# A hybrid GLA and DeltaNet layer: a substitution's transfers on GpSimd's queue, and a reordered last scaling

## The chip, the cores and the metric

The kernel runs on one core of one Trainium2 chip. The metric is the device time of one execution in microseconds (us); the median of several executions counts. The core has five engines that run their own instruction lists in order: PE (TensorE, matrix products, with its weight loads shown as PEld), DVE (VectorE), ACT (ScalarE), POOL (GpSimd) and SP (SyncE). SP, ACT and POOL can also issue transfers (DMA); such an issue stands in the engine's own list, and an issue that has to wait holds back whatever stands behind it on that engine.

## The reference, cut to what matters

```python
h = rms_norm(x, g_mix); z = h @ w_in                       # 256 tokens, 2048 channels
o_gla = gla_mixer(...)                                     # 4 heads
# gated delta rule, 16 heads, chunks of 64 tokens
a = where(strict, (k_beta @ k.T) * decay, 0)
t_mat = triangular_solve(eye + a, eye, lower, unit_diagonal)
u, w = t_mat @ (v * beta), t_mat @ (k_beta * exp(gcum))    # then a scan over the chunks
x = x + mixed @ w_out
x = x + square(relu(rms_norm(x, g_mlp) @ w_up)) @ w_down
x = x + sigmoid(rms_norm(x, g_ple) @ w_ple_gate) * (p @ w_ple_proj)
out = rms_norm(x, g_final)                                 # x * rsqrt(mean(x*x)+eps) * g_final
```

## The kernel before, in words

All matrix products keep fp32 accuracy by splitting each operand into two parts. A helper, `weights`, loads 1 MB of weights into a tile `raw` (line 93, issued by SP), rounds it to `whi` on ACT (line 101) and subtracts to `wlo` on DVE (line 102). One such pair of tiles feeds one group of matmuls: in `stream` 12 matmuls of 512 columns (lines 114 to 116). There are three buffers each of `raw`, `whi` and `wlo`, so ACT and DVE can be three groups ahead of PE and no more. A matmul on line 114 needs `whi` of its group, the next one, on line 115, needs `wlo`.

The mixers run in four passes of the loop over `h` (line 353), each with one GLA head and four DeltaNet heads. In each pass the inverse of the triangular matrices is built from 32x32 diagonal blocks, for which the kernel does a forward substitution with one block per partition (lines 465 to 492):

- Four transfers (line 468) write the diagonal blocks of the tile `af` to a DRAM tile `da`; one (line 470) reads it back as `a32`, which is a slice of the buffer `cacc`.
- 62 small DVE instructions (lines 479 and 481) do the substitution into `t32`, between the DVE work of the streams; a copy (line 483) puts the transposed result into `cacc` again.
- `t32` goes to DRAM as `dt` (line 484), the copy as `du` (line 485); from there two transfers fill `t11` (line 491), four `u_bd` (line 489), one `tb` (line 492). These are read by small matmuls (lines 574 and 582) some 40 us later.

The buffer `cacc` exists once. Its next user is the convolution of the same pass's V: `qkv("v", ...)` starts it with four ACT instructions (line 378), each followed by three DVE instructions (line 381, 12 in all), which end in one ACT instruction (line 384). So line 378 cannot start before the transfer `du` has read `cacc`, that is, before it has landed.

At the end (lines 808 to 845) the gate product is done for 512 columns at a time, the last 512 columns for each half of the tokens in two blocks of 256 columns (96 matmuls of 256 columns for each 128 tokens). `gated` evacuates a block: sigmoid on ACT (801), two DVE instructions (802, 803), a sum of squares on ACT (804), and a DVE product with `gfin` (806), the final gain. Then the sum, the root on POOL (178), four scalings by it, two on DVE (844) and two on ACT (842), and four transfers out by SP (845).

The order of the instructions on each engine is set at build time by a scheduler that works with its own estimates of durations. Where an instruction is given to another engine, the scheduler also orders the others anew.

Of the kernel before, what the change touches and what calls it, by code (L numbers as in the profile page):

```python
# [12 lines left out]
AF = mybir.ActivationFunctionType  # L13
ALU = mybir.AluOpType
AX = mybir.AxisListType
# [3 lines left out]
D = 2048  # L19
# [18 lines left out]
def hybrid_block(ctx: ExitStack, tc: tile.TileContext, A: dict, out: bass.AP):  # L38
    nc = tc.nc
    V, SC, GP, TE, SY = nc.vector, nc.scalar, nc.gpsimd, nc.tensor, nc.sync  # L40
# [27 lines left out]
    def mm():  # L68

        return psm.tile([P, 2, 512], F32, tag="mm", name="mm")  # L70
# [4 lines left out]
    def T4(tag, bufs=None, dt=F32):  # L75
        return mp.tile([P, 4, S], dt, tag=tag, bufs=bufs, name=tag)
# [98 lines left out]
    def rsqrt_(dst, src, mul, tmp):  # L175

        V.tensor_scalar(tmp, src, mul, EPS, ALU.mult, ALU.add)
        GP.tensor_tensor(dst, tmp, mhalf[:, :dst.shape[1]], ALU.pow)
# [101 lines left out]
    rtmp = const.tile([P, NT], F32, name="rtmp")  # L280
# [18 lines left out]
    u_bd = mp.tile([P, 8, P], F32, name="u_bd")  # L299
    t11 = mp.tile([64, 8, 64], F32, name="t11")  # L300
# [52 lines left out]
    for h in range(GH):  # L353
# [58 lines left out]
        for i, src in enumerate((kT, qT)):  # L412
            for t in range(NT):
# [4 lines left out]
                for hd in range(4):  # L418
                    c = i * 8 + t * 4 + hd
# [22 lines left out]
        af = T4("af").rearrange("p a (b c) -> p (a b) c", b=2)  # L442
        for t in range(NT):
            ts = slice(t * P, (t + 1) * P)
# [20 lines left out]
        da, dt_, du = (dram.tile([32, 32, 32], F32, name=n) for n in ("da", "dt", "du"))  # L465
        for b in range(4):
            bs = slice(b * 32, (b + 1) * 32)
            SC.dma_start(da[b * 8:(b + 1) * 8].rearrange("i s c -> s i c"), af[bs, :, bs])
        a32 = T4("cacc")[0:32].rearrange("p a b -> p (a b)").rearrange("p (s c) -> p s c", s=32)
        SC.dma_start(a32, da)  # L470
        t32 = mp.tile([P, NT, 512], F32, tag="og", name="t32").rearrange("p a b -> p (a b)")[0:32]
        GP.memset(t32, 0.0)
        GP.memset(t32[:, 0:1024:33], 1.0)
        t32 = t32.rearrange("p (c s) -> p c s", c=32)
        tmp = mp.tile([P, 8, 32], F32, tag="tmp", name="tmp").rearrange("p a b -> p (a b)")[0:32]
        for j in range(31):
            n, m = 31 - j, j + 1
# [3 lines left out]
            V.tensor_tensor(t32[:, j + 1:, 0:m], t32[:, j + 1:, 0:m], tv, ALU.subtract)  # L481
        u32 = a32
        V.tensor_copy(u32, t32.rearrange("p c s -> p s c"))
        SC.dma_start(dt_, t32)
        SC.dma_start(du, u32)
        tb = mp.tile([P, 8, 32], F32, tag="tmp", name="tb")
        for b in range(4):
            bs, ds = slice(b * 32, (b + 1) * 32), slice(b * 8, (b + 1) * 8)
            SC.dma_start(u_bd[bs, :, bs], du[ds].rearrange("i s c -> s i c"))  # L489
            if b < 2:  # L490
                SC.dma_start(t11[bs, :, bs], dt_[ds].rearrange("i c s -> c i s"))
        SC.dma_start(tb[64:96], dt_[16:24].rearrange("i c s -> c i s"))

        vT = qkv("v", O_DV, 32)
        rv = mp.tile([P, NT, 4, P], F32, name="rv")
# [30 lines left out]
        for t in range(NT):  # L526
            ts = slice(t * P, (t + 1) * P)
# [153 lines left out]
        for kp in range(2):  # L681
            pz = mx3(2, S)
            for kk in range(2):
                for t in range(NT):
                    c = (kp * 2 + kk) * P
# [8 lines left out]
    x_sb = late.tile([P, NT, D], F32, name="x_sb")  # L694
# [79 lines left out]
    gfin = late.tile([P, D], F32, name="gfin")  # L774
# [12 lines left out]
    def ple_proj(n):  # L787
        pj = [None, None]

        def ev(t, ps):  # L790
            pj[t] = late.tile([P, 512], F32, tag=f"pj{t}", name="pj")
            SC.activation(pj[t], ps, AF.Copy)

        stream([w_pp[:, n * 512:(n + 1) * 512]], 2, pT, ev)
        return pj

    def gated(t, c, n, ps, pj, i):

        xs = x_sb[:, t, c:c + n]
        s = late.tile([P, 512], F32, tag="u", bufs=2, name="s")[:, 0:n]  # L800
        SC.activation(s, ps, AF.Sigmoid, scale=r3[:, t:t + 1])
        V.tensor_tensor(s, s, pj, ALU.mult)
        V.tensor_tensor(xs, xs, s, ALU.add)
        SC.activation(late.tile([P, 512], F32, tag="junk", name="junk")[:, 0:n], xs, AF.Square,
                      accum_out=ssf[:, t, i:i + 1])
        V.tensor_tensor(xs, xs, gfin[:, c:c + n], ALU.mult)

    ssf = late.tile([P, NT, 5], F32, name="ssf")
    for n in range(3):
        pj = ple_proj(n)  # L810
        stream([w_pg[:, n * 512:(n + 1) * 512]], KD, h3T,
               lambda t, ps: gated(t, n * 512, 512, ps, pj[t], n))


    pj = ple_proj(3)
# [8 lines left out]
    ssl = late.tile([P, NT], F32, name="ssl")  # L824
    r4 = late.tile([P, NT], F32, name="r4")
    for t in range(NT):
        ts = slice(t * P, (t + 1) * P)
        for half in range(2):
            cs = slice(half * 256, (half + 1) * 256)
            ps = mm()[:, 0, 0:256]  # L830
            for k in range(KD):
                hi, lo = kept[k]
                TE.matmul(ps, h3T[0][:, k, ts], hi[:, cs], start=(k == 0), stop=False)
                TE.matmul(ps, h3T[0][:, k, ts], lo[:, cs], start=False, stop=False)
                TE.matmul(ps, h3T[1][:, k, ts], hi[:, cs], start=False, stop=(k == KD - 1))
            gated(t, 1536 + half * 256, 256, ps, pj[t][:, cs], 3 + half)
        V.reduce_sum(ssl[:, t:t + 1], ssf[:, t, :], axis=AX.X)
        rsqrt_(r4[:, t:t + 1], ssl[:, t:t + 1], 1.0 / D, rtmp[:, t:t + 1])
        for n in range(4):
            xs = x_sb[:, t, n * 512:(n + 1) * 512]  # L840
            if n % 2:
                SC.activation(xs, xs, AF.Copy, scale=r4[:, t:t + 1])
            else:
                V.tensor_scalar(xs, xs, r4[:, t:t + 1], None, ALU.mult)
            SY.dma_start(out[0, ts, n * 512:(n + 1) * 512], xs)


_INS = ["x", "p", "g_mix", "w_in", "gla_w2", "gla_b", "gla_norm", "dn_conv", "dn_a_log", "dn_dt_bias", "dn_norm",
# [19 lines left out]
```

## Time and profile before

| | |
|---|---|
| median of 3 runs | 1858.05 us (1855.92 to 1859.32) |
| the profiled execution | 1857.95 us, of which the span of the instructions is 1856.2 us |
| PE busy | 1827.8 us, 98% of the span |
| DVE, ACT, POOL busy | 64%, 51%, 4% |
| DMA | 334 MB, 180 GB/s in the mean |

The span is what the views of the trace show; 1.75 us of the execution lie outside it. PE's busy time is the sum of its records, whose ends are modelled; matmuls follow each other faster than one record lasts, so what PE loses is best read from the starts of neighbouring matmuls. PEclk is the granted clock of TensorE, 1.00 being 2.4 GHz.

### The profile page before, as it was taken

Reading aid. Unit: us, or ns where it says so; the run is one execution under the profiler, and the core shown is the slowest. Engines: PE = TensorE matmul, PEld = TensorE weight load, DVE = VectorE, ACT = ScalarE, POOL = GpSimd, SP = SyncE. Lnnn points to the kernel's source line nnn. Section 1 sums busy time; section 2 is a strip of 40 time slices with the busy share of each in tenths; the row PEclk is TensorE's granted clock in tenths of the full one; section 3 lists DMA queues with packets and bytes.
Section 4 is the critical chain, followed back from the end, with each engine's and each line's share of the span. In section 5 each row is a group of like instructions: output and inputs, shape, how many; then the busy total and the mean of one; then the engine's idle time right before and its main releaser. Section 6 shows DMA issues by size and latency. Waiting matters only on the chain.

```text
span 1856.2 us, 24598 instructions
## 1 busy us (share of the span) xinstructions
PE 1827.8 (98%) x9796; PEld 1551.0 (84%) x9796; DVE 1180.2 (64%) x1637; ACT 946.6 (51%) x1324; POOL 77.5 (4%) x100
## 2 busy tenths in 40 slices
PE   8999999999999999999999999999999999999998
PEld 7887888878888788887888888888888888888887
DVE  5686577864768647686455655555556555565665
ACT  6745556455564655645545544444444434344654
POOL 3110011000110001100000000000000000000000
PEclk9999999999999999999999999999999999999999
DMA  7555446554455545565465665656656565655453
GB/s 239 148 185 169 159 149 192 168 172 160 155 179 187 178 150 159 159 205 167 144 233 191 184 192 182 198 187 188 196 183 194 191 190 193 187 188 195 162 201 137
DMA packets 245236, 334.02 MB, mean 180 GB/s; under 512 B 21680, under 2 KB 148992, under 8 KB 244736
## 3 DMA queue, kind: packets, MB, share of 16 engines
q1 hardware_dynamic: 231488, 325.47, 54.4%
q10 hardware_dynamic: 12992, 4.34, 1.0%
q0 software_dynamic: 640, 2.63, 0.4%
q8 instruction: 77, 1.26, 0.3%
q14 instruction: 39, 0.32, 0.0%
HBM read 328.74 MB, written 3.67 MB: 179 GB/s over the span
## 4 chain that ended last, share of the span: by engine, by line
PE 92%; DMA 3%; DVE 2%; ACT 2%; issue 1%; ACTq 1%; SPq 0%; POOLq 0%; POOL 0%; DVEq 0%
PE mm L131 24%; PE mm L115 16%; PE mm L116 16%; PE mm L114 16%; PE mm L135 13%; DMA du<-cacc 1%; DMA raw<-in_w_in 1%; PE mx L457 1%; DMA x_sb<-in_x 1%; DVE wlo L102 1%; ACT whi L101 1%; DVE cacc L381 1%; PE mx L562 0%; PE mx L168 0%; ACTq L489 0%
## 5 line engine op out<-in xcount | busy, mean ns | idle before, releaser
L102 DVE TENSOR_TENSOR wlo<-raw,whi 128x1024 fp32r<-128x1024 f32 x604 | 743.8, 1234 | 532.0 <-ACT whi L101 523.3
L101 ACT ACTIVATE whi<-raw 128x1024 fp32r<-128x1024 f32 x604 | 638.8, 1060 | 746.5 <-PE mm L116 389.3
L131 PE MATMUL mm<-act,whi 128*128 128x512 f32 x1984 | 542.7, 395 | 0.0
L131 PEld LDWEIGHTS mm<-act,whi 128*128 128x128 f32 x1984 | 339.7, 189 | 45.8
L115 PE MATMUL mm<-wlo,act 128*128 128x512 f32 x864 | 343.1, 397 | 8.9 <-DVE wlo L102 8.9
L114 PE MATMUL mm<-whi,act 128*128 128x512 f32 x864 | 339.2, 393 | 3.2 <-ACT whi L101 3.2
L135 PEld LDWEIGHTS mm<-act,wlo 128*128 128x128 f32 x1984 | 304.0, 189 | 43.0 <-issue 1.0
L116 PE MATMUL mm<-whi,act 128*128 128x512 f32 x864 | 338.9, 392 | 0.0
L135 PE MATMUL mm<-act,wlo 128*128 128x256 f32 x1984 | 317.4, 281 | 0.0
L115 PEld LDWEIGHTS mm<-wlo,act 128*128 128x128 f32 x864 | 163.1, 189 | 44.0 <-DVE wlo L102 10.4
L116 PE MATMUL mm<-whi,ul 128*128 128x512 f32 x512 | 199.6, 390 | 0.0
L114 PE MATMUL mm<-whi,uh 128*128 128x512 f32 x512 | 199.5, 390 | 0.0
L115 PE MATMUL mm<-wlo,uh 128*128 128x512 f32 x512 | 199.3, 389 | 0.0
L114 PEld LDWEIGHTS mm<-whi,act 128*128 128x128 f32 x864 | 162.8, 188 | 38.3 <-ACT whi L101 4.9
L116 PEld LDWEIGHTS mm<-whi,act 128*128 128x128 f32 x864 | 163.1, 189 | 33.7 <-issue 1.0
L116 PEld LDWEIGHTS mm<-whi,ul 128*128 128x128 f32 x512 | 96.1, 188 | 19.9
L115 PEld LDWEIGHTS mm<-wlo,uh 128*128 128x128 f32 x512 | 96.1, 188 | 19.8
L114 PEld LDWEIGHTS mm<-whi,uh 128*128 128x128 f32 x512 | 96.1, 188 | 19.6
L381 DVE SCALAR_TENSOR_TENSOR cacc<-zT,convw,cacc 128x255 f32<-128x255 f32 (+2 forms) x144 | 61.0, 477 | 18.0 <-ACT cacc L378 18.0
L757 DVE SCALAR_TENSOR_TENSOR x_sb<-mm,r2sq,x_sb 128x512 f32<-128x512 f32 x64 | 45.1, 746 | 12.2 <-PE mm L116 12.2
L479 DVE TENSOR_TENSOR tmp<-cacc,t 32x31 f32<-32x31 f32 (+15 forms) x124 | 40.6, 328 | 4.4 <-DMA cacc<-da 1.5
L481 DVE TENSOR_TENSOR t<-t,tmp 32x31 f32<-32x31 f32 (+15 forms) x124 | 40.8, 329 | 2.8
(311 smaller groups left out, 1230.6 us busy)
## 6 DMA issues: line engine op xcount, KB each, us to landing
raw<-in_w_in SPq DMA_DIRECT2D x143, 1024.0 KB, 4.9
raw<-in_w_up SPq DMA_DIRECT2D x64, 1024.0 KB, 5.6
raw<-in_w_down SPq DMA_DIRECT2D x64, 1024.0 KB, 4.9
raw<-in_w_out SPq DMA_DIRECT2D x16, 1024.0 KB, 4.9
raw<-in_w_ple_gate SPq DMA_DIRECT2D x16, 1024.0 KB, 4.9
x_sb<-in_x POOLq DMA_DIRECT2D x1, 2048.0 KB, 12.4
raw<-in_w_ple_proj SPq DMA_DIRECT2D x4, 512.0 KB, 3.8
out<-x_sb SPq DMA_DIRECT2D x8, 256.0 KB, 2.5
```

The costliest lines, as they stand in the source:

```text
L101: SC.activation(hi[:, :, :c], raw[:, kk:kk + g, :c], AF.Copy)
L102: V.tensor_tensor(lo[:, :, :c], raw[:, kk:kk + g, :c], hi[:, :, :c].bitcast(F32), ALU.subtract)
L114: TE.matmul(pt[:, t, :n], xh[:, k, ts], hi, start=(k == 0), stop=False)
L115: TE.matmul(pt[:, t, :n], xh[:, k, ts], lo, start=False, stop=False)
L116: TE.matmul(pt[:, t, :n], xl[:, k, ts], hi, start=False, stop=(k == nk - 1))
L131: TE.matmul(pt[c // 2][:, c % 2, :], hi[:, c * P:(c + 1) * P], xx[:, k].rearrange("p a s -> p (a s)"), start=(k == 0), stop=False)
L135: TE.matmul(pt[c // 2][:, c % 2, S:2 * S], lo[:, c * P:(c + 1) * P], xh[:, k, :], start=False, stop=(k == nk - 1))
L381: V.scalar_tensor_tensor(acc[:, hd, sh:], zt[:, hd, :S - sh], w(i), acc[:, hd, sh:], ALU.mult, ALU.add)
L457: TE.matmul(pk[:, hd, :], kT[:, hd, ts], rhs[:, hd, ts], start=True, stop=True)
L479: V.tensor_tensor(tv, a32[:, j, j + 1:].unsqueeze(2).to_broadcast([32, n, m]), t32[:, j, 0:m].unsqueeze(1).to_broadcast([32, n, m]), ALU.mult)
L481: V.tensor_tensor(t32[:, j + 1:, 0:m], t32[:, j + 1:, 0:m], tv, ALU.subtract)
L757: V.scalar_tensor_tensor(x_sb[:, t, ns], ps, r2sq[:, t:t + 1], x_sb[:, t, ns], ALU.mult, ALU.add)
```

## The change

All transfers of the substitution are issued by GpSimd (`GP`) and no longer by ScalarE (`SC`). In the last part the first 128 tokens take the last 512 columns in one block. The gain `g_final` is no longer multiplied in by `gated` for the last columns (all 512 of the first 128 tokens, the last 256 of the second); one DVE instruction does the root and the gain together for these, and is first in the last scaling. The four scalings and four transfers out are put in another order, and one of the four is issued by ACT.

```diff
-            SC.dma_start(da[b * 8:(b + 1) * 8].rearrange("i s c -> s i c"), af[bs, :, bs])
+            GP.dma_start(da[b * 8:(b + 1) * 8].rearrange("i s c -> s i c"), af[bs, :, bs])
         a32 = T4("cacc")[0:32].rearrange("p a b -> p (a b)").rearrange("p (s c) -> p s c", s=32)
-        SC.dma_start(a32, da)
+        GP.dma_start(a32, da)
...
         V.tensor_copy(u32, t32.rearrange("p c s -> p s c"))
-        SC.dma_start(dt_, t32)
-        SC.dma_start(du, u32)
+        GP.dma_start(dt_, t32)
+        GP.dma_start(du, u32)
...
-            SC.dma_start(u_bd[bs, :, bs], du[ds].rearrange("i s c -> s i c"))
+            GP.dma_start(u_bd[bs, :, bs], du[ds].rearrange("i s c -> s i c"))
             if b < 2:
-                SC.dma_start(t11[bs, :, bs], dt_[ds].rearrange("i c s -> c i s"))
-        SC.dma_start(tb[64:96], dt_[16:24].rearrange("i c s -> c i s"))
+                GP.dma_start(t11[bs, :, bs], dt_[ds].rearrange("i c s -> c i s"))
+        GP.dma_start(tb[64:96], dt_[16:24].rearrange("i c s -> c i s"))
...
-        V.tensor_tensor(xs, xs, gfin[:, c:c + n], ALU.mult)
+        if gain:
+            V.tensor_tensor(xs, xs, gfin[:, c:c + n], ALU.mult)
...
-        for half in range(2):
-            cs = slice(half * 256, (half + 1) * 256)
-            ps = mm()[:, 0, 0:256]
+        w = 256 if t else 512
+        for i, c in enumerate(range(0, 512, w)):
+            cs = slice(c, c + w)
+            ps = mm()[:, 0, 0:w]
...
-            gated(t, 1536 + half * 256, 256, ps, pj[t][:, cs], 3 + half)
-        V.reduce_sum(ssl[:, t:t + 1], ssf[:, t, :], axis=AX.X)
-        rsqrt_(r4[:, t:t + 1], ssl[:, t:t + 1], 1.0 / D, rtmp[:, t:t + 1])
-        for n in range(4):
-            xs = x_sb[:, t, n * 512:(n + 1) * 512]
-            if n % 2:
-                SC.activation(xs, xs, AF.Copy, scale=r4[:, t:t + 1])
+            gated(t, 1536 + c, w, ps, pj[t][:, cs], 3 + i, gain=c < 256 and t == 1)
+        V.reduce_sum(ssl[:, t:t + 1], ssf[:, t, 0:4 + t], axis=AX.X)
+        r = r4[:, t:t + 1]
+        rsqrt_(r, ssl[:, t:t + 1], 1.0 / D, rtmp[:, t:t + 1])
+        xs = lambda c, n: x_sb[:, t, c:c + n]
+        V.scalar_tensor_tensor(xs(2048 - w, w), xs(2048 - w, w), r, gfin[:, 2048 - w:2048], ALU.mult, ALU.mult)
+        if t:
+            SC.activation(xs(1536, 256), xs(1536, 256), AF.Copy, scale=r)
+        SY.dma_start(out[0, ts, 1536:2048], xs(1536, 512))
+        for n in (1, 0, 2):
+            if n == 1:
+                SC.activation(xs(n * 512, 512), xs(n * 512, 512), AF.Copy, scale=r)
             else:
-                V.tensor_scalar(xs, xs, r4[:, t:t + 1], None, ALU.mult)
-            SY.dma_start(out[0, ts, n * 512:(n + 1) * 512], xs)
+                V.tensor_scalar(xs(n * 512, 512), xs(n * 512, 512), r, None, ALU.mult)
+            (SC if n == 1 else SY).dma_start(out[0, ts, n * 512:(n + 1) * 512], xs(n * 512, 512))
```

What the scheduler makes of it is shown at three places, all in the second pass of the loop over `h`. First ACT, behind the two evacuations of line 521: before,

```order
L101 ACTIVATE whi<-raw 128x1024 x5
L484 DMA dt<-t_2928 32x1024
L485 DMA du<-cacc 32x1024
L101 ACTIVATE whi<-raw 128x1024
L491 DMA t_118<-dt 32x8x32
L489 DMA u_bd<-du 32x8x32 x2
L491 DMA t_118<-dt 32x8x32
L489 DMA u_bd<-du 32x8x32 x2
L492 DMA tb<-dt 32x8x32
L378 ACTIVATE cacc<-zT,convw 128x256 x4
L101 ACTIVATE whi<-raw 128x1024 x2
L655 ACT_TABLE_LOAD
```

and now:

```order
L101 ACTIVATE whi<-raw 128x1024 x8
L378 ACTIVATE cacc<-zT,convw 128x256 x4
L655 ACT_TABLE_LOAD
L655 ACTIVATE gate_3879<-mm,r_114 128x512
L655 ACTIVATE gate_3881<-mm,r_114 128x512
L101 ACTIVATE whi<-raw 128x1024 x3
L384 ACTIVATE Tv<-cacc 128x1024
```

The issues are gone from ACT; eight and no longer six roundings stand ahead of line 378, and the next one stands behind the table load and the two evacuations of line 655. The other passes read the same.

Second DVE, at the end of the substitution: before,

```order
L102 TENSOR_TENSOR wlo<-raw,whi 128x1024
L479 TENSOR_TENSOR tmp<-cacc,t_2928 32x31
L481 TENSOR_TENSOR t_2928<-t_2928,tmp 32x31
L483 COPY cacc<-t_2928 32x1024
L102 TENSOR_TENSOR wlo<-raw,whi 128x1024 x2
L381 SCALAR_TENSOR_TENSOR cacc<-zT,convw,cacc 128x255 x2
```

and now:

```order
L479 TENSOR_TENSOR tmp<-cacc,t_2928 32x31
L102 TENSOR_TENSOR wlo<-raw,whi 128x1024
L481 TENSOR_TENSOR t_2928<-t_2928,tmp 32x31
L483 COPY cacc<-t_2928 32x1024
L102 TENSOR_TENSOR wlo<-raw,whi 128x1024 x2
L381 SCALAR_TENSOR_TENSOR cacc<-zT,convw,cacc 128x255 x2
```

Counted from the start of the stream, the instruction of line 102 ahead of the copy is now that of the sixth group (`whi` tile) behind line 521, and was that of the fourth (of the fifth in the first pass): the copy has moved behind two more groups (one more in the first pass). Third POOL, now:

```order
L461 TENSOR_TENSOR at<-at,m_incl 128x512
L468 DMA da<-af 32x8x32 x4
L461 TENSOR_TENSOR at<-at,m_incl 128x512
L470 DMA cacc<-da 32x1024
L484 DMA dt<-t_2928 32x1024
L485 DMA du<-cacc 32x1024
L491 DMA t_118<-dt 32x8x32 x2
L492 DMA tb<-dt 32x8x32
L489 DMA u_bd<-du 32x8x32 x4
L549 MEMSET ga_5532 128x128
```

Before, the two instructions of line 461 stood there next to each other, and then line 549.

## Rows read from the trace of the kernel before

**Rows 1.** Busy time by stretches of 25 us: PE, PEld, DVE, ACT, POOL, then PEclk, DMA.
```profile
150.00:175.00 25.00, 22.26 (x91) 17.76 (x90) 18.43 (x37) 12.65 (x16) 0.00 (x0) 0.93 0.59 171
...
375.00:400.00 25.00, 22.26 (x97) 17.86 (x96) 17.50 (x35) 12.79 (x16) 0.00 (x0) 1.00 0.62 188
...
625.00:650.00 25.00, 22.39 (x109) 18.52 (x108) 16.39 (x27) 18.39 (x32) 0.00 (x0) 1.00 0.46 149
...
850.00:875.00 25.00, 21.29 (x92) 17.19 (x91) 13.78 (x23) 17.80 (x32) 0.00 (x0) 0.93 0.41 129
```
**Rows 2.** Timeline of PE, second pass: start, length, instruction, idle before and releaser.
```profile
396.14 0.39 PE L115 MATMUL mm<-wlo,act 128*128 128x512 f32 x1
396.37 0.39 PE L116 MATMUL mm<-whi,act 128*128 128x512 f32 x1
397.42 0.50 PE L114 MATMUL mm<-whi,act 128*128 128x512 f32 x1 [0.66 <-ACT whi L101]
400.09 0.50 PE L115 MATMUL mm<-wlo,act 128*128 128x512 f32 x1 [2.17 <-DVE wlo L102]
```
**Rows 3.** Timeline of DVE, second pass.
```profile
385.86 1.14 DVE L483 COPY cacc<-t 32x1024 f32<-32x1024 f32 x1
...
389.79 1.23 DVE L102 TENSOR_TENSOR wlo<-raw,whi 128x1024 fp32r<-128x1024 f32 x1 [1.55 <-ACT whi L101]
395.26 3.65 DVE L381 SCALAR_TENSOR_TENSOR cacc<-zT,convw,cacc 128x255 f32<-128x255 f32 x9 [4.24 <-ACT cacc L378]
398.82 1.22 DVE L102 TENSOR_TENSOR wlo<-raw,whi 128x1024 fp32r<-128x1024 f32 x1
```
**Rows 4.** Timeline of ACT, second pass (ACTq: its transfer issues).
```profile
387.02 0.31 ACTq L485 DMA_DIRECT2D du<-cacc  x1
388.70 1.06 ACT L101 ACTIVATE whi<-raw 128x1024 fp32r<-128x1024 f32 x1 [1.71 <-PE mm L116]
...
394.71 1.71 ACT L378 ACTIVATE cacc<-zT,convw 128x256 f32<-128x256 f32 x4 [4.96 <-issue]
396.33 1.99 ACT L101 ACTIVATE whi<-raw 128x1024 fp32r<-128x1024 f32 x2
398.33 1.28 ACT L655 ACT_TABLE_LOAD   x1
...
400.79 1.06 ACT L101 ACTIVATE whi<-raw 128x1024 fp32r<-128x1024 f32 x1
```
**Rows 5.** All instructions of line 485: time from issue to landing, over four passes.
```profile
DMA to landing us min/median/max: 1.9/4.5/5.2
```
**Rows 6.** Transfers issued by POOL at the start: name, KB, us to landing.
```profile
gnw<-in_gla_norm POOLq DMA_DIRECT2D x1, 256.0 KB, 8.7
vec<-in_dn_conv POOLq DMA_DIRECT2D x1, 64.0 KB, 5.6
dnw<-in_dn_norm POOLq DMA_DIRECT2D x1, 64.0 KB, 6.9
...
dtb<-in_dn_dt_bias POOLq DMA_DIRECT2D x1, 8.0 KB, 5.0
```
**Rows 7.** Timeline of ACT and DVE, first pass: the substitution's first transfers.
```profile
107.03 1.85 ACTq L468 DMA_DIRECT2D da<-af  x4
...
114.00 0.18 DVE L479 TENSOR_TENSOR tmp<-cacc,t 32x31 f32<-32x31 f32 x1 [1.54 <-DMA cacc<-da]
```
**Rows 8.** Timeline of POOL: the longest of its eleven transfer issues.
```profile
958.52 0.82 POOL L695 DMA_DIRECT2D x_sb<-in_x  x1 [13.98 <-ACT whi L101]
```
**Rows 9.** Timeline of PE at the end.
```profile
1846.95 0.28 PE L834 MATMUL mm<-ul,act 128*128 128x256 f32 x1
1847.07 0.28 PE L835 MATMUL mm<-act 128*128 128x256 f32 x1
```
**Rows 10.** Timeline of DVE at the end.
```profile
1849.42 0.42 DVE L806 TENSOR_TENSOR x_sb<-x_sb,gfin 128x256 f32<-128x256 f32 x1 [0.63 <-ACT junk L804]
1849.76 0.15 DVE L837 TENSOR_REDUCE ssl<-ssf 128x1 f32<-128x5 f32 x1
```

More of the change, by code (lines that the diff above doesn't have):

```diff
@@ L795, in ple_proj, with gated @@
         return pj
-    def gated(t, c, n, ps, pj, i):
+    def gated(t, c, n, ps, pj, i, gain=True):
         xs = x_sb[:, t, c:c + n]
```

## The prediction

> **What bounds the kernel now.** I read the table first: PE is busy for 98% of the span, so only what makes PE wait counts. The windows of 25 us over the whole span then give the places. PE is short of 25.00 in four of them, one in each pass of the loop over `h` [rows 1]: 2.74, 2.74, 2.61 and 3.71 us, together 11.8. The timeline of PE shows such a place in the second pass [rows 2]: the starts 396.37, 397.42 and 400.09 are 1.05 and 2.67 apart where a matmul takes 0.23 (396.14 to 396.37), so 3.27 us are lost there and not the 2.74 of the window, whose records end too late. With 0.5 more for each place the four lose 13.8 us. Two of the windows also have a granted clock of 0.93: 7% of 25 us, or 1.75 us, at full speed. The levels are 1.2 and 2.4 GHz, so that is 3.5 us at the lower one, in the same window as the wait; some of it falls in the wait itself, so I count 1.5 for each, 3.0. **All four places cost 16.8 us.**
>
> What PE waits for is read backwards: on `wlo` of line 102 [rows 2], which stood on DVE behind nine instructions of line 381 (395.26 to 398.82), which waited 4.24 us for line 378 on ACT [rows 3]. Line 378 started at 394.71 after 4.96 us in which ACT had only issues in hand [rows 4]: those of lines 491, 489 and 492, which wait for `dt` and `du` to land. `du` was issued at 387.02, and such a transfer lands after 1.9 to 5.2 us, 4.5 in the median [rows 5]. Meanwhile no `whi` was rounded, and PE used up what it had ahead.
>
> **The change, part by part.** *The issues leave ACT.* The next rounding then goes on as soon as PE frees a `whi`, and the four waits above, as they are, go: up to 16.8 us. But line 378 still needs `cacc`, that is `du` landed, and everything behind it on ACT waits with it: the rounding of the ninth group, the table load and two evacuations of line 655. So the same stall can come back three groups later.
>
> *When `du` is issued.* The copy of line 483 now stands behind line 102 of the sixth group. That one started at 389.79 when `whi` came [rows 3], and takes about 1.14 (1.23 as recorded, its neighbours overlap); `du` can't be sooner than 389.79 + 1.14 + 0.22 (line 481) + 1.14 (line 483, [rows 3]) = 392.3, 5.3 us later than now.
>
> *What the ninth group needs.* From the start of line 378: its four instructions 1.62 (394.71 to 396.33), the table load and both evacuations 2.46 (398.33 to 400.79), the rounding 1.06 [rows 4], line 102 1.22, some 0.1 between engines: 6.45. (Line 381 on DVE has twelve instructions of about 0.4, 4.9 from the first, and is done by then.) PE without a wait would go on from 396.60 with the seventh group, and would need `wlo` of the ninth at 396.60 + 2 x 2.72 + 0.23 = 402.27 (12 x 0.227 = 2.72 per group). The stall is therefore 392.3 + du + 6.45 − 402.27 = **du − 3.5**, where du is the time from POOL's issue to landing. In the first pass the copy moves by one group and not two; the same working gives du − 3.1. Four passes: **4 du − 13.6**, and nothing where du is below about 3.4.
>
> *What du is on POOL's queue.* No transfer of this kind is issued by POOL in this trace. The nearest rows are its loads at the start [rows 6]: 5.0 us for 8 KB, 5.6 and 6.9 for 64 KB, 8.7 for 256 KB; `du` has 128 KB. From below there is the same transfer on ACT's queue, 1.9 at best. Size puts it between 64 and 256 KB; the loads of the start however go beside the program's first weights, and around `du` the transfers' share is 0.4 to 0.6 [rows 1]. I take **6.0**, between the smallest load and the slower of 64 KB. Then the stalls are 2.9 + 3 x 2.5 = 10.4 us. Of the four stalls now, two (2.74 and 3.71) have a slow clock beside them and two have not; for the shorter new ones I add half of one such spell, 0.75. The exchange is −16.8 + 11.15 = **−5.65**.
>
> A rule bears on this. The Trainium skill, in "DMA: Bandwidth & Descriptors", section "Anatomy of one DMA — SWDGE (gpsimd) path", fits a transfer from GpSimd as about 2.0 us and its bytes at 436 GB/s, which makes 2.3 for `du`, an estimate from that page. The trace does not agree: its smallest load from there took 5.0 [rows 6]. By the page no stall would come back and the time would be 1840.2, by the rows it is 1851.3.
>
> *The first transfers of a pass.* `da` and `a32` also take the slower queue. In the first pass ACT issued `da` from 107.03 on and line 479 started at 114.00 [rows 7]. POOL's issues take up to 0.82 [rows 8], so the last of four is out by 110.3; two landings of 5 to 5.5 later it is about 121. DVE has other work of its list until about 117 and then idles some 3 to 4 us. Line 102 is up to three groups of 2.72 ahead there, by my replay of the new order with 1.1 us left at an idle time of 2.7; so this costs between 0 and about 1 us in that pass, and nothing in the others, where 3 us and more are left. I take 0. The transfers into `u_bd`, `t11` and `tb` are read some 40 us after their issue and have 20 us to spare: 0. POOL's issues themselves stand ahead of a `memset` of line 549 that is needed tens of us later: 0.
>
> *The end.* The first 128 tokens' last block is 48 matmuls of 512 columns, 48 x 0.227 = 10.9 us, instead of 96 of 256, which follow each other by 0.12 [rows 9] and take 11.5: −0.63. For the last block of the second half line 806 (0.42 recorded, 0.34 from 1849.42 to 1849.76) leaves the way to the sum of line 837 [rows 10]; the gain joins a scaling that is made anyway: −0.34. The outputs leave in another order, 1 MB either way, with one issue by ACT: 0, give or take 0.3. Together **−0.97**.
>
> Sum: 1857.95 (the profiled execution, which is 0.1 below the median of 1858.05) − 5.65 − 0.97 = **1851.3**.
>
> **The rivals.** *POOL's queue is quick enough.* If the loads at the start were slow because they were first or because of the weights beside them, `du` takes what it takes on ACT, 1.9 to 4.5 [rows 5]. Up to 3.4 there is no stall: 1857.95 − 16.8 − 0.97 = 1840.2; at 4.5 the stalls are 4.4 and the time is 1844.6. Against it speaks that not one POOL load was under 5.0. Chance 0.20.
>
> *The stall returns in full.* With du at 6.6 to 8.0 the new stalls (12.8 to 18.4, and one or two slow spells of 1.5) cost what the old ones did: 1854.3 to 1861.8. `du` is queued right behind `dt`, of the same size, and 64 KB took up to 6.9. Chance 0.22.
>
> *The kernel gets slower.* Place: line 378 in each pass; point: du above about 8.0. At the 8.7 of 256 KB [rows 6] the stalls are 4 x 8.7 − 13.6 = 21.2, the clock falls in two of them (3.0), and the exchange is +7.4: 1857.95 + 7.4 − 0.97 = 1864.4. DVE's work could bring it there by holding back what POOL has to write for a transfer; the only issue beside DVE's line 102 took 0.82 [rows 8], no more than ordinary, which speaks against it. Chance 0.16. The Trainium skill has this rule: "SBUF — State Buffer", section "Summary: rules for kernel authors", says that descriptors of GpSimd's transfers are starved while DVE is in a fast mode, and advises ACT or SP as issuers. No row here shows it; by the page alone this rival would be the forecast.
>
> **How the numbers follow.** The forecast (du 5.0 to 6.6) has 0.42, with times of its own from 4 x 5.0 − 13.6 = 6.4, so 1847.3, to 1854.5 with a whole slow spell. Something like 0.2%, 3.7 us, is what a measurement of this kernel can tell from no change: faster is below 1854.3, slower above 1861.8. So faster 0.42 + 0.20, same 0.22, slower 0.16. The range goes from the middle of the quick case, 1841.5, to 1862.5, just inside the slow one, and leaves out some 0.06 below and 0.12 above.
>
> **What would show it.** In the profile after, ACT's idle time should end before line 378 with the landing of `du`, the start of 378 lying du behind POOL's issue, and PE should wait on line 114 or 115 of the ninth group, by du − 3.5. The time from issue to landing of line 485 decides all: 5 to 6.6 is right, 4 or less is the quick rival, 8 or more the slow one. The windows should show four places with about 2 us short of 25 and at most one granted clock below 1.00. Line 479 of the first pass should wait about 3 us for `a32`, with no PE wait behind it; if PE waits there, that step is wrong. At the end 48 matmuls of 512 columns and no line 806 before line 837. Prediction and cause are wrong if ACT is free at line 378 and PE still waits at these four places, or if POOL issues `du` more than 1 us behind line 483.

## The result, and the profile after

The changed kernel takes 1845.45 us in the median (1844.5 to 1847.06, 4 runs) beside 1858.68 us of the kernel before in the same comparison: a ratio of 0.993, 95% interval 0.991 to 0.995, so faster by 0.7%. The time lies in the range that was given, 6 us below the forecast of 1851.3. The profiled execution took 1847.06 us, the slowest of the four.

The windows over the same stretches as [rows 1] (PE, PEld, DVE, ACT, POOL busy, PEclk, DMA):

```profile
150.00:175.00 25.00, 24.71 (x109) 19.95 (x107) 20.37 (x40) 13.33 (x17) 5.53 (x9) 1.00 0.62 203
375.00:400.00 25.00, 25.00 (x112) 20.70 (x111) 20.12 (x39) 12.72 (x16) 5.27 (x9) 1.00 0.68 222
400.00:425.00 25.00, 24.21 (x119) 19.80 (x118) 13.41 (x20) 17.33 (x33) 0.21 (x1) 1.00 0.49 163
625.00:650.00 25.00, 24.03 (x119) 19.65 (x118) 14.57 (x23) 17.32 (x33) 0.72 (x2) 1.00 0.48 151
850.00:875.00 25.00, 24.19 (x120) 19.80 (x119) 15.82 (x27) 17.56 (x32) 1.76 (x4) 1.00 0.49 162
```

The holes of 2.6 to 3.7 us are gone, new ones of 0.3 to 1.0 us have come at the ninth group instead of the seventh, and the granted clock is 1.00 throughout. PE's timeline shows the new hole of the second pass, beside [rows 2]:

```profile
399.57 0.39 PE L114 MATMUL mm<-whi,act 128*128 128x512 f32 x1
399.79 0.39 PE L115 MATMUL mm<-wlo,act 128*128 128x512 f32 x1
400.02 0.39 PE L116 MATMUL mm<-whi,act 128*128 128x512 f32 x1
400.44 0.50 PE L114 MATMUL mm<-whi,act 128*128 128x512 f32 x1
401.70 0.50 PE L115 MATMUL mm<-wlo,act 128*128 128x512 f32 x1 [0.76 <-DVE wlo L102]
```

The starts are 0.42, 1.26 and (to the next matmul) 0.33 apart where 0.23 is usual: 1.33 us lost, again for `wlo`. Added up in this way, the four passes lose 1.23, 1.33, 1.53 and 1.36, together 5.45. ACT's timeline shows why, beside [rows 4], and POOL's shows when `dt` and `du` were issued:

```profile
395.15 1.71 ACT L378 ACTIVATE cacc<-zT,convw 128x256 f32<-128x256 f32 x4 [1.80 <-DMA du<-cacc]
396.87 1.28 ACT L655 ACT_TABLE_LOAD   x1
398.17 1.27 ACT L655 ACTIVATE gate<-mm,r 128x512 f32<-128x512 f32 x2
399.32 2.95 ACT L101 ACTIVATE whi<-raw 128x1024 fp32r<-128x1024 f32 x3
```
```profile
389.81 0.71 POOL L484 DMA_DIRECT2D dt<-t  x1 [52.12 <-issue]
390.71 0.49 POOL L485 DMA_DIRECT2D du<-cacc  x1 [0.19 <-issue]
```

Line 378 waits for `du`: it starts 4.44 us behind `du`'s issue and 0.1 behind its landing, and `whi` of the ninth group comes behind the table load and line 655, at about 400.4. All four `du` (line 485), as [rows 5] before:

```profile
DMA to landing us min/median/max: 3.8/4.4/4.6
```

Where the difference of the two profiled spans (1856.2 − 1845.3 = 10.9) comes from is read from the starts of matmuls with the same number in PE's list, at places where both lists have done the same work:

| stretch | after against before, us |
|---|---|
| first 95 us, before any changed instruction runs | +1.9 |
| first, second and third pass, fourth pass and a little more | −3.64, −2.34, −1.95, −4.53 |
| to PE's last matmul | −0.82 |
| PE's last matmul to the end of the span | +0.50 |

The first line is how one execution differs from another (the same stretch of a second profile of the changed kernel was 2.0 us shorter). The passes bring 12.46. With the 5.45 of new losses, 17.9 us of old ones (holes and slow clock) have gone.

### The profile page after: what moved, and what is told of

Read it like the earlier page. It is cut to its first block, busy times and chain, and to the rows that moved or that the text cites. A ratio compares the mean times of both kernels' runs of the same rounds, so it can differ in the third digit from the quotient of the medians.

```text
span 1845.3 us, 24528 instructions
## 1 busy us (share of the span) xinstructions
PE 1825.5 (99%) x9748; PEld 1547.8 (84%) x9748; DVE 1182.8 (64%) x1634; ACT 946.1 (51%) x1320; POOL 112.2 (6%) x156
## 3 DMA queue, kind: packets, MB, share of 16 engines
q8 instruction: 76, 1.25, 0.3%
## 4 chain that ended last, share of the span: by engine, by line
PE 82%; issue 12%; DMA 3%; ACT 2%; DVE 1%; POOL 0%; SPq 0%; POOLq 0%; DVEq 0%; ACTq 0%
PE mm L131 23%; PE mm L115 14%; PE mm L116 13%; PE mm L114 13%; PE mm L135 11%; DMA du<-cacc 1%; DMA raw<-in_w_in 1%; DMA x_sb<-in_x 1%; PE mx L457 1%; ACT whi L101 0%; PE mx L168 0%; PE mx L562 0%; DVE wlo L102 0%; PE mm L150 0%; PE mm L149 0%
```

## The experiments

Times are medians; the ratio is to the kernel before, run beside each. "Loss" is what neighbouring starts of matmuls show above 0.23 us.

**Parts of the change alone.** `e1_queue_only` is the kernel before with the diff of the substitution, `e2_end_only` the kernel before with the diff of lines 797 to 845.

> Only the transfers change queue; the end is as before. Theory: the gain is made in the four passes alone. The starts of neighbouring matmuls lose about 1.0 us at the ninth group in each pass (1.4 in the third) and nothing at the places of before, so the passes bring about 12.3 us; POOL's closing DRAIN takes about 6.2 us as in the whole change and ends some 0.8 us behind SP's last wait, so the net is about -11.5 us against before, near 0.994. Rival (a good part of the gain comes from the end): -9 us or less, and a DRAIN of 1.6 us.

1846.77 us, 0.993 (0.991 to 0.995). The passes bring 12.3 us in its profile, PE loses 1.3 to 1.7 us at each ninth group, POOL's DRAIN takes 6.16 us. The passes and the DRAIN are as the theory said; the losses are 0.2 to 0.6 us larger than it had them, and the time is 14.5 us below before and not 11.5 (the interval of the ratio holds both).

> Only the end changes; the transfers stay on ACT's queue. Theory: the four places of before stay as they are (about 3.2 us each, 4.2 in the fourth, with slow-clock spells in some), PE's last matmul comes about 0.8 us earlier, the sum of squares to the root 0.34 earlier, POOL's DRAIN stays at 1.6 us and nothing waits for it: about -1.2 us against before, which is within 0.2%. Rival (the reordered end lengthens the DRAIN): 6 us of DRAIN, and no gain at all.

1860.2 us against 1861.25, 0.9995 (0.998 to 1.001): no measurable difference, as expected. The four holes are those of before (2.9 to 3.9 us at lines 114 and 115), the DRAIN is 1.58 us. So the whole measurable gain is the queue's.

**`du` from a buffer of its own.** In the whole change and in the kernel before:

```diff
-        u32 = a32
+        u32 = mp.tile([P, NT, 4, P], F32, tag="rv", name="u32").rearrange("p a b c -> p (a b c)")[0:32]
+        u32 = u32.rearrange("p (s c) -> p s c", s=32)
```

> The whole change, and the copy that du is read from goes into a buffer of its own (that of rv) and no longer into cacc, so line 378 need not wait for du. Theory: the remaining stalls of about 1.0, 1.0, 1.4 and 1.0 us go, with nothing in their place: 4.4 us less than the whole change, about 1841 us or 0.991 of before. Rival (PE waits there because POOL's transfers or issues hold something else up, not for cacc): the stalls stay, 1845.5 us.

1842.38 us, 0.990 (0.989 to 0.992). No loss is left at the ninth groups, so the new stalls are line 378's wait for `cacc`. Beside the whole change this is 3.1 us less (the starts of matmuls in the passes say 3.0), so some 1.3 of the expected 4.4 us are missing; this profile has a wait of 1.25 us that the whole change has not, at line 135 near 258 us:

```profile
258.05 0.62 PE L135 MATMUL mm<-act,wlo 128*128 128x256 f32 x3 [1.09 <-DVE wlo L102]
```

> The kernel before, with only the copy that du is read from in a buffer of its own (that of rv); the issues stay on ACT. Theory (what bound the kernel before was ACT standing at the issues of lines 491, 489 and 492 and not cacc): ACT still stands until about 0.5 us behind the last of these issues, some 7.6 us behind the issue of du, and then does line 384 and its table load first; PE loses about 2.6 us or more in each pass where it lost 3.3, and the time is within 3 us of before. Rival (cacc alone held ACT): no stall of PE is left in the passes and the time falls by 12 us or more.

1843.48 us, 0.991 (0.989 to 0.993): the time is the rival's. ACT's timeline of the second pass however is the theory's:

```profile
382.40 0.31 ACTq L486 DMA_DIRECT2D du<-u  x1
...
386.72 0.32 ACTq L492 DMA_DIRECT2D t<-dt  x1
387.09 0.96 ACTq L490 DMA_DIRECT2D u_bd<-du  x2
388.08 0.47 ACTq L492 DMA_DIRECT2D t<-dt  x1
388.59 0.99 ACTq L490 DMA_DIRECT2D u_bd<-du  x2
389.61 0.47 ACTq L493 DMA_DIRECT2D tb<-dt  x1
390.17 1.28 ACT L384 ACT_TABLE_LOAD   x1 [5.01 <-DVE cacc L381]
```

ACT stands at the issues until 390.1, 7.8 us behind `du`'s, as before (394.71 − 387.02 = 7.7 in [rows 4]); line 381, named as the releaser, ended at 389.4. What differs is on PE:

```profile
391.85 0.39 PE L116 MATMUL mm<-whi,act 128*128 128x512 f32 x1
392.57 1.09 PE L500 MATMUL mx<-ident,Tv 128*128 128x128 f32 x8 [0.34 <-ACT Tv L384]
...
394.19 0.40 PE L114 MATMUL mm<-whi,act 128*128 128x512 f32 x1
394.78 0.50 PE L115 MATMUL mm<-wlo,act 128*128 128x512 f32 x1 [0.19 <-DVE wlo L102]
```

With the convolution done before the wait, `Tv` is ready at once, and the transposes of line 500 with four matmuls of line 533 fill 1.6 us of the hole (392.57 to 394.19). PE loses 0.50 + 0.36 and no more than that, and no low clock follows. So the theory had ACT's wait right and what PE has to do meanwhile wrong: "ACT waits" and "PE waits" are two different prices.

**Which issues must leave ACT.** `e6_loads_only` gives back to ACT the writes and `a32`, `e8_writes_only` the loads; `e7_loads_only_own` is `e6_loads_only` with the buffer of its own.

```diff
-            GP.dma_start(da[b * 8:(b + 1) * 8].rearrange("i s c -> s i c"), af[bs, :, bs])
+            SC.dma_start(da[b * 8:(b + 1) * 8].rearrange("i s c -> s i c"), af[bs, :, bs])
```

The same in `e6_loads_only` and `e7_loads_only_own` for `a32`, `dt_` and `du`. In `e8_writes_only`, and the same there for `t11` and `tb`:

```diff
-            GP.dma_start(u_bd[bs, :, bs], du[ds].rearrange("i s c -> s i c"))
+            SC.dma_start(u_bd[bs, :, bs], du[ds].rearrange("i s c -> s i c"))
```

> The whole change, but the writes (da, dt, du) and the load of a32 are issued by ACT again, and only the loads of t11, u_bd and tb, which wait for the writes, by POOL; du is read from cacc as in both kernels. Theory (what held ACT in the kernel before was standing at the issues of these loads and their own length; du's landing alone comes soon enough, as the copy stands as early as before): line 378 starts when du lands, some 3 us earlier than before, the first wait of PE shrinks from 3.3 us to at most 0.3 in a pass, and the one behind the ninth group is gone too; the DRAIN is 4.0 us with 39 transfers and hidden behind the outputs. About 4.7 us less than the whole change: 1841. Rival (the landing of du is what counts, whoever issues): stalls of 2 us and more in each pass, 1849 or slower.

1843.33 us, 0.991 (0.989 to 0.992). Line 378 starts when `du` has landed and there is no loss at the ninth groups, though `du` lands no sooner here than in the other kernels (median 4.4): it is issued sooner, since the copy stands where it stood before. PE loses 0.9 us once, in the fourth pass, and there is a 1.25 us wait at line 135 as in `e3_own_u32`; so some 2 us were won and not 4.7. The two medians come from different comparisons whose intervals overlap; in the profiles the passes bring 14.0 us here and 12.5 in the whole change.

> The whole change, but the loads of t11, u_bd and tb are issued by ACT again, and only the writes and a32 by POOL. Theory (the issues of the loads, behind du's landing, take ACT some 3.1 us more before line 378): line 378 starts 3.1 us later than in the whole change, PE waits about 4.1 us at the ninth group of each pass, 16 us in all and perhaps a slow-clock spell, DRAIN 4.0 us: 1857 to 1860, no better than before. Rival (only du's landing counts): as the whole change, 1845.

1871.32 us, 1.006 (1.004 to 1.007): slower than before, by more than expected. The second pass on ACT:

```profile
397.77 1.06 ACT L101 ACTIVATE whi<-raw 128x1024 fp32r<-128x1024 f32 x1 [1.66 <-PE mm L116]
400.36 0.31 ACTq L491 DMA_DIRECT2D t<-dt  x1
...
403.38 0.41 ACTq L492 DMA_DIRECT2D tb<-dt  x1
403.84 1.71 ACT L378 ACTIVATE cacc<-zT,convw 128x256 f32<-128x256 f32 x4 [5.01 <-issue]
```

The seven issues take 3.4 us (3.1 expected) from the landing of `dt` at 400.3 on; `du` landed at 400.7, so line 378 starts 3.2 us behind it. The loss at the ninth group is 4.4 in this pass, and in its window the clock falls, as in two of [rows 1]:

```profile
400.00:425.00 25.00, 21.00 (x84) 16.96 (x84) 13.06 (x25) 16.88 (x31) 0.00 (x0) 0.86 0.45 136
```

A clock 0.14 short over 25 us is 3.5 us at full speed; a spell of this kind or of half its size (0.93) follows in each pass, where the expectation had one at most. Three waits of 1.25 us at line 135 come on top.

> As e6_loads_only, and du is read from a buffer of its own. Theory: nothing on ACT waits for a transfer any more between the streams; no PE wait over 0.3 us in the places of both kernels, DRAIN 4.0 us and hidden: about 1840, within 1.5 us of e6_loads_only and 2 us faster than e3_own_u32. Rival (own buffer and POOL's loads cover the same wait twice and the scheduler's new order costs something else): 1842 to 1844, no better than e3_own_u32 or e4_before_own_u32.

1840.41 us, 0.989 (0.988 to 0.991), the fastest here, and 2.0 below `e3_own_u32`, as the theory said. It is 2.9 below `e6_loads_only`, where the theory had at most 1.5: the wait at line 135 and the loss in the fourth pass are gone too. Windows of the second pass and the hole's place in the fourth:

```profile
375.00:400.00 25.00, 25.00 (x116) 20.73 (x116) 18.45 (x33) 17.00 (x26) 4.12 (x7) 1.00 0.63 197
...
825.00:850.00 25.00, 25.00 (x116) 20.73 (x116) 18.68 (x33) 16.78 (x26) 4.12 (x7) 1.00 0.64 199
```

**Why `du` takes 4.4 us.** In the whole change SP issues 1 MB of weights some 0.6 us before `dt`. The DMA queues from `dt`'s issue (389.8) to 393.4, and from there to `du`'s landing (q1 is SP's, q0 POOL's):

```profile
q1 hardware_dynamic: 452, 0.93, 85.2%
```
```profile
q0 software_dynamic: 96, 0.26, 38.5%
q1 hardware_dynamic: 76, 0.12, 19.1%
```

Not one packet of POOL's moves until 452 of the load have; in the four passes 460 to 491 of the load's packets start before POOL's first, and `du` lands 0.6 to 0.7 us behind the load. In `e3_own_u32`, where `du` goes out some 2 us behind the load's issue and not 1.5, it takes 3.5 in the median. In `e9_sp_writes` SP issues `dt` and `du` itself; in `e11_writes_first` an ordering edge also puts the next load behind `du`.

```diff
-        GP.dma_start(dt_, t32)
-        GP.dma_start(du, u32)
+        SY.dma_start(dt_, t32)
+        SY.dma_start(du, u32)
```

and in the second, in place of the last of these lines and in `weights`:

```diff
+        late_du.update(du=SY.dma_start(du, u32).ins, n=0)
...
+                    late_du["n"] = late_du.get("n", 0) + (w == NCH)
+                    behind = "du" in late_du and w == NCH and late_du["n"] == 11
+                    with tc.issue_after(late_du["du"]) if behind else ExitStack():
                         SY.dma_start(raw[:, ka:ka + step, cc:cc + s.shape[1]],
```

> The whole change, but dt and du are issued by SP, in its list ahead of the 1 MB load of weights that in the whole change is issued just before them; ACT's and DVE's lists read as in the whole change. Theory (du takes 4.4 us on POOL's queue not because of that queue, but because some 450 packets of SP's load, issued 0.6 us before dt, go first): du lands within 2 us of its issue, below the 3.4 at which no stall is left; the waits of PE at the ninth groups (1.0, 1.0, 1.4, 1.0 us) go, the DRAIN is 5.5 us with 55 transfers and costs 0.1; the load that comes 1.5 us later is not missed. About 5 us less than the whole change, 1840.5. Rival (the writing of 128 KB from 32 partitions itself takes 4.4): the stalls stay, about 1845.

1846.69 us, 0.993 (0.992 to 0.994), as the whole change, and `du` lands after 4.2 to 4.8 us. This decides nothing, because the list still has the load ahead: its second 1 MB of the first row below was issued 0.5 us before `dt`.

```profile
DMA to landing us min/median/max: 4.2/4.6/4.8
```
```profile
382.98 5.81 SPq L93 DMA_DIRECT2D raw<-in_w_in  x2
388.88 0.45 SPq L484 DMA_DIRECT2D dt<-t  x1
389.67 0.32 SPq L485 DMA_DIRECT2D du<-cacc  x1
```

> As e9_sp_writes, but the load of weights that stood in SP's list right ahead of dt is now ordered behind du (in e9_sp_writes the list still had it ahead, so that run could not tell). Theory (du's 4.4 us is the wait for that load's packets): the packets of dt follow its issue within 1.5 us, du lands about 2 us after its issue in all four passes, line 378 has no wait left, and the losses at the ninth groups are gone: about 1841. Rival (the write itself, or the time of the pass at which it comes, takes 4.4): du lands after more than 4 us in passes 2 to 4 as in every kernel so far.

SP's list now, and line 490 (`du`), in all four passes:

```profile
382.35 0.37 SPq L98 DMA_DIRECT2D raw<-in_w_in  x1
387.92 0.33 SPq L489 DMA_DIRECT2D dt<-t  x1
389.03 0.32 SPq L490 DMA_DIRECT2D du<-cacc  x1
389.44 7.39 SPq L98 DMA_DIRECT2D raw<-in_w_in  x2
```
```profile
DMA to landing us min/median/max: 1.9/2.0/2.0
```

This settles the landing on SP's queue: 2.0 us where the last load was issued 5.6 us before `dt`, 4.6 where it was issued 0.5 before. The losses at the ninth groups are gone. The time is 1846.36 us, 0.992 (0.991 to 0.994), not the 1841 expected: waits of 1.25 us at line 140 (135 of the other kernels) in the second and third pass, 0.44 in the first, and more between 925 and 975 us. The DVE timeline at one of them:

```profile
480.48 1.53 DVE L671 TENSOR_TENSOR gate<-gate,dnw 128x512 f32<-128x512 f32 x1
481.93 1.00 DVE L650 TENSOR_SCALAR ms<-ms 128x8 f32<-128x8 f32 x1
482.85 0.68 DVE L671 TENSOR_TENSOR gate<-gate,dnw 128x512 f32<-128x512 f32 x1
483.45 2.35 DVE L107 TENSOR_TENSOR wlo<-raw,whi 128x1024 fp32r<-128x1024 f32 x2
```

The scheduler, which places everything anew after each edit, has put the output gate's instructions ahead of two `wlo`; the same stand before the 1.25 us waits of `e3_own_u32`, `e6_loads_only` and `e8_writes_only`. Two of them are also long, 1.53 and 1.00 where the same instructions take 0.69 and 0.17 at other places, and both run beside POOL's masks (line 454; line 449 in the whole change):

```profile
481.43 1.48 POOL L454 TENSOR_TENSOR sig<-m_incl,ggl 128x512 fp32r<-128x512 f32 x1
```

In this kernel, the whole change and `e7_loads_only_own`, every one of DVE's gate products and small instructions there that lies beside these masks for 0.97 us or more is 0.84 us longer than the rest. How much of the 1.25 us is due to that was not tested. These waits explain some 4 us; what else this kernel loses against `e7_loads_only_own` stays open.

> The whole change once more, on the same chip as e9_sp_writes, for the comparison. All theories: 1845.5 us within 2 us, stalls of 1.0 us in three passes and 1.4 in the third (by what the starts of matmuls lose), DRAIN 6.2 us.

1844.78 us, 0.992 (0.990 to 0.993), beside `e9_sp_writes`: losses of 1.3 to 1.5 at the ninth groups (0.1 to 0.4 more than expected), DRAIN 6.16.

> e7_loads_only_own once more, on the same chip as e11_writes_first, to compare the two fastest. Theory: both have no wait of PE left at the places of before, so they lie within 2 us of each other, 1840 to 1842. Rival (SP's late load costs PE waits elsewhere, as the 0.44 us that e9_sp_writes had at line 135 in three passes): e11_writes_first is 2 us slower or more.

1840.2 us, 0.989 (0.988 to 0.991), beside `e11_writes_first`, which is 6 us slower: the rival's time holds. Its reason, SP's late load, is not what the DVE rows above show, where `wlo` waits for DVE's own list.

**The end of POOL.** The last line of the table of stretches, +0.50, is 0.34 won to the root and 0.8 lost behind it: SP has seen its last output at 1843.8, but the closing barrier waits for POOL, whose DRAIN (line 871; line 864 before) starts with the last root at 1838.4. Before, after, and in `e6_loads_only`:

```profile
L864 POOLq DRAIN  x3: 46/93/1583, 1850.1 to 1856.0; - x3
```
```profile
L871 POOLq DRAIN  x3: 46/102/6157, 1838.4 to 1845.1; - x3
```
```profile
L871 POOLq DRAIN  x3: 46/102/3870, 1834.5 to 1840.6; - x3
```

`e5_52_more` adds 52 transfers on POOL that nothing waits for:

```diff
+    scr = dram.tile([52, 8], F32, name="scr")
+    for k in range(52):
+        GP.dma_start(scr[k:k + 1, :], mhalf[0:1, 0:8])
     ssf = late.tile([P, NT, 5], F32, name="ssf")
```

> The whole change, and 52 more transfers of 32 bytes each from a constant to DRAM, issued by POOL in the quiet second half, which nothing waits for. POOL's closing DRAIN took 1.58 us with 11 transfers issued by POOL in the program and 6.16 us with 63, that is 0.088 us for each. Theory (the DRAIN grows with the number of POOL's transfers, whenever they were issued): 10.7 us of DRAIN with 115 transfers, and the end 4.6 us later than in the whole change, about 1850. Rival (it grows with bytes, or with the packets of the substitution, or waits for something at the end): 6.2 us and 1845.5 us.

The counts in the expectations are too low by four where POOL issues the writes, as a pass has 14 of these transfers and not 13: the traces have 67 in the whole change (not 63), 119 here (not 115) and 59 in `e9_sp_writes` (not 55); 11 before and 39 in `e6_loads_only` are right.

```profile
L874 POOLq DRAIN  x3: 46/102/10403, 1845.4 to 1856.3; - x3
```

10.4 us (10.7 expected), 5 of them behind SP's last wait. 1854.49 us, 0.997 (0.995 to 0.998), some 4 us above the expected time: the scheduler put the 52 issues not into the second half but between 12 and 73 us, and the stretch up to 95 us is 7 us longer in this profile. That they were done by 100 us and still lengthen the DRAIN at 1845 makes the point more strongly. Neither bytes nor packets set its length: `e6_loads_only` and `e8_writes_only` both have 39 transfers on POOL, with 1536 and 1728 packets and 3.55 and 4.73 MB, and both DRAINs take 3.87 us.

## Why the prediction was right, and where its size was off

**The place and the mechanism** held. The waits on ACT went, line 378 then waited for `du`, and PE for the ninth group's `wlo`. The windows, the timeline of line 378 and `e3_own_u32`, in which the wait on `cacc` is taken away, show it. The old places were worth 17.9 and not 16.8 us. The starts of matmuls before give 13.6 for the holes (13.8 in the prediction), 0.4 for a gap of 0.1 behind each, which had not been counted, and 1.3 and 1.6 for the slow clock in the first and fourth pass (1.5 each in the prediction), where five and eight matmuls in a row start 0.43 apart instead of 0.23; the other 0.9 is not assigned. The fourth pass before, with the granted clock at 0.72 in these 6 us and 0.50, the level of 1.2 GHz, from 859.2 to 862.5:

```profile
858.00:864.00 6.00, 6.00 (x20) 4.78 (x21) 3.87 (x6) 3.67 (x5) 0.00 (x0) 0.72 0.54 175
```

**The term that was mis-sized is du: 6.0 against 4.4.** The step that failed is taking POOL's loads of the program's start [rows 6] as the price of that queue. The wait is for what is queued on the DMA engines, not for who issues: behind a load issued some 1.5 us earlier 4.4 to 4.6 in the median on ACT's, POOL's and SP's queue alike, 1.9 to 2.0 where the load had been issued more than 4 us earlier (SP in `e11_writes_first`, ACT in the first pass of before, the 1.9 of [rows 5]). No run has `du` on POOL's queue without such a load; the nearest is POOL's `da` below. So du of 4.5, which the prediction had given to the rival "quick enough" at 1844.6, is what came; that the time still lies in the range is because the range took in that rival. With 3.8, 4.4, 4.6 and 4.4 the formula gives 0.7, 0.9, 1.1 and 0.9; measured were 1.23, 1.33, 1.53 and 1.36. Of the 0.4 more, 0.3 in the second pass is POOL's issue of `dt`, behind which `du` went out 0.3 us after its copy had ended (389.29 + 1.12 against 390.71); 0.1 lies between the landing and line 378.

The fit of the Trainium skill ("DMA: Bandwidth & Descriptors", section "Anatomy of one DMA — SWDGE (gpsimd) path"), by which the estimate for `du` was 2.3 us, has no term for a load that is queued ahead. The trace agrees with it only where there is none just before: POOL's `da`, 32 KB (2.1 by the fit, an estimate), lands in 1.9 to 2.5 us in the last three passes, where SP's load was issued 4 us and more before, and in 2.6 to 3.9 in the first, 1.3 to 3.2 us behind a load.

The other rule that was weighed, of the Trainium skill ("SBUF — State Buffer", section "Summary: rules for kernel authors"), that DVE in a fast mode starves GpSimd's transfers, no run here shows. While `du` was on its way in the second pass, DVE worked for 2.4 of 4.35 us (line 102, twice), and `du` landed as soon from POOL as from SP behind the same load (4.4 and 4.6 in the median). No view shows in which mode DVE was, so this is no test of the rule.

**The slow clock** was counted with 0.75 and did not come: all windows of the passes are at 1.00 after losses of 1.2 to 1.5 us. Losses of 4.4 and more in `e8_writes_only` were followed by it every time; of the four holes before, those of 3.2 and 4.2 were, and those of 3.3 and 3.0 were not, so the size of the loss alone does not decide.

**The first transfers.** Line 479 of the first pass waits 0.85 us for `a32`, not some 3, and PE does not wait behind it:

```profile
119.59 0.18 DVE L479 TENSOR_TENSOR tmp<-cacc,t 32x31 f32<-32x31 f32 x1 [0.85 <-DMA cacc<-da]
```

**The end.** PE's part was 0.82 (0.63 forecast) and the root's 0.34 as forecast, but POOL's DRAIN takes back 0.8, which no term had. Neither is measurable (`e2_end_only`). With the measured terms the sum is 1857.95 − 12.46 (passes) − 0.82 + 0.50 (end) = 1845.2, which is the profiled 1847.06 less the 1.9 by which its first 95 us were longer.

**The slower rival** had its point right, though not by POOL's queue: `e8_writes_only` starts line 378 3.2 us behind `du`'s landing and is slower than before.

## What to carry to other kernels

A transfer that one engine issues and the next step waits for costs what is queued ahead of it on the DMA engines (2.0 us here, and 4.4 to 4.6 right behind 1 MB): before pricing it, look in the queue view at what was issued in the two microseconds before it. Move to an idle queue the issues that have to *wait* (the loads behind a write), and leave on the busy engine those that are ready at once. The first half is shown (`e8_writes_only`, the reverse, is slower than before); the second half brought some 2 us here, not clear of the noise, and the scheduler's earlier copy of line 483 has a part in it. And give a short-lived copy its own buffer before arguing about queues (that alone, on the kernel before, brought as much as the whole change). Where a scheduler orders the lists, read the new order of every engine after each edit: four of these kernels lost 1.25 us at a time to instructions that had nothing to do with it.

## What was not expected of the hardware

POOL's closing DRAIN grows with the number of transfers that POOL has issued in the whole program, however early and small: 1.58 us for 11, 3.87 for 39, 5.50 for 59, 6.16 for 67, 10.40 for 119, which is 0.082 us for each further one at every step. It costs time once it outlasts the output, here from about 58 transfers on: SP was done with its last wait 0.1 us before the DRAIN's end with 59, 0.8 with 67 and 5.0 with 119.
